# Three small edits to a hybrid decoder step: the pace of gating beside cross attention, the engine of one row scaling, the priority of one subtraction

## The chip, the cores and the metric

The kernel runs on one core of a Trainium2 chip. A core has five engines with instruction queues of their own: TensorE (PE, matrix products; PEld in the profile are its weight loads), VectorE (DVE), ScalarE (ACT), GpSimd (POOL) and SyncE (SP, which here only issues DMAs). Each engine works off its queue in order; semaphores make one wait for another. The metric is the time of one execution on the device in microseconds, as the median of several runs.

## The reference

One layer of a decoder, for a prompt of 1024 rows and for 8 samples with one new row each, all float32:

```python
# prompt
q, k, v, logf, u, z = mixer_inputs(rmsnorm(xp, g_mix), w_in, b_f, g_sgu_v)
xp = xp + merge_heads(fox_prompt(q, k, v, logf), sgu_prompt(u, z, w_s, b_s), g_att_out, g_sgu_out, w_o)
mk, mv = memory_kv(mem_prompt, g_mem, w_ck, w_cv)
xp = xp + cross_attend(rmsnorm(xp, g_cross), mk, mv, w_cq, w_co)
f, conv_p = conv_ffn(rmsnorm(xp, g_ffn), zeros, w_up, conv_w, conv_b, w_down)
y_prompt = rmsnorm(xp + f, g_final)
# samples: the same layer, with fox_sample over 8192 cached keys and values per sample
c = cumsum(concatenate([logf_cache, logf_new]))           # sums of the gates
s = q . k * 64 ** -0.5 + (c[query] - c[key])
att = softmax(s) @ v
```

The model width is 1024 and the feed-forward width 2816. Attention has 8 heads of 64, the spatial gating unit (`sgu`) 8 heads of 64 that mix the 128 rows of a chunk, and cross attention 4 heads of 256 over 256 memory rows. The gating unit computes u * (w_s z + b_s) for each chunk; its result is normed by rows, joins the attention output and goes through w_o.

## The kernel before

**Two streams.** The kernel is built as two Python generators. `prompt()` issues the work on the 1024 rows; `sample()` issues the decode of the 8 samples, whose caches are gathered page by page. Each `yield` of a number says how much PE time, roughly, has just been issued. A loop at the end of `build` adds these numbers up, and each time that a pace (`PACE`, by phase; 8.0 in the phase mid0) is reached, it issues one more step of the decode. While `held[0]` is set, no decode step is issued.

**Two halves.** The prompt is worked in two halves of 512 rows, four tiles of 128 rows each. The order is: input projection (`p1`), attention of half 0 and half 1, and then for each half: merge and output projection w_o, cross attention (`cross`), feed-forward (`ffn`). A product in float32 is made as three matmuls of high and low parts (`gemm3`, lines 272 to 274); `split` makes the parts, the high one on ACT (L235 or L238) and the low one on DVE (L236 or L239).

**Who sets the order.** The instructions are not run in the order in which the code issues them. A planner places them: it goes through the engines in modelled time and gives each engine the ready instruction with the first place in the code, as soon as a buffer for its result is free. Inside `with tc.high_priority():` an instruction gets a place ahead of all ordinary ones, so it is taken as soon as it is ready. `tc.issue_after(x)` and `behind(engine)` keep instructions behind another one of the same engine. The chip then runs each engine's list in that fixed order.

**Buffers.** Large row tiles come from `U`: 18 buffers of 128x1024 float32 values. The tiles of `xt` (4 buffers per half), the transposed and split inputs `hs` and `ls` (8), the query blocks `q2` (one per head), the probabilities `pp` (one per head), their transposes `pT`, and gating's `wst`, `z` and `u` all take one each. The bank `ms` of PSUM exists once (`MS`), and is shared by the decode and by attention.

**Gating.** `gating(hf)` computes the gating unit of one half in eight steps, each ending in `yield 1`. Steps one to three treat the first pair of chunks: the loads of w_s, z and u (L631, L638, L639), the scaling of z (L641), then twice four matmuls (L649) and four products with u (L659). Step four squares the first pair's rows on ACT (L230) and begins the second pair, with its loads; steps five and six are its matmuls and products; step seven squares its rows and makes the row factors (L222 on DVE, L223 on POOL); step eight scales the rows on DVE (L678) and stores them to `sgn_d` (L679). Half 0's gating runs beside attention. Half 1's runs beside half 0's cross attention, by `mix(cross(xt, sq), gating(1), 0.05)`: after each yield of d of the main stream, d times the ratio is added to an account, and gating steps are issued while it is above zero, each taking 1 off. What is left when the main stream ends is issued right behind it.

**Cross attention's yields.** `norm_T` yields 8 x 0.6 + 3 = 7.8, the query projections 8 x 5.2 = 41.6, the steps of the four heads 26, and `out_proj` 8 x 2.6 + 4 x 0.1 + 4 x 5.2 = 42: in all 117.4. In `cross`, the projection of the queries fills `q2` (L1226, ACT); `weigh` makes the scores (L1180), their maxima (L1182, DVE), the exponentials (L1188, ACT) and the scaling by the sums (L1193, ACT); `turned` and `gather` transpose the probabilities and multiply them with the memory values (L1200, L1208).

**The end of cross attention.** `out_proj` multiplies with w_co, column half by column half. In the second column half tiles 0 and 1 come one by one, tiles 2 and 3 together (L1082 to L1084). `residual` adds x (L1016, DVE) and squares the rows (L230, ACT); `factor` makes 1/rms of a tile (L1032 on ACT, L1033 on POOL). `both` then scales tiles 2 and 3 by their factors, half by half (L1045, L1046), for the transposes of the feed-forward's `norm_T` (L1116) and its first product (`gemm3_late`, L280 to L284). `both` is called once for each half of the prompt.

**The decode's gates.** For each sample, `gates_scan` sums the gates within a page and `gates` across pages: two small sums on PE into the bank `ms` (L1410), and on DVE a subtraction of 128x512 values (L1412) that reads this bank and writes `dec`. `soft_max` adds `dec` to the scores two steps later.

Of the kernel before, what the change touches and what calls it, by code (L numbers as in the profile page):

```python
# [11 lines left out]
AF = mybir.ActivationFunctionType  # L12
ALU = mybir.AluOpType
# [5 lines left out]
P = 128  # L19
# [59 lines left out]
def build(nc, tc, ctx, a, phases=None):  # L79
# [31 lines left out]
    def U(shape, dt=F32):  # L111
        n = 1
        for s in shape[1:]:
            n *= s
        t = upool.tile([P, UW], dt, tag="u", bufs=NU, name=nm("u"))[:, :n]
        if len(shape) == 3:
            t = t.rearrange("p (a b) -> p a b", b=shape[2])
        return t
# [7 lines left out]
    def sm(shape, tag, bufs=2, dt=F32):  # L126
        return small.tile(shape, dt, tag=tag, bufs=bufs, name=nm(tag))
# [136 lines left out]
    def wpair(w, kk, c0, n):  # L264

        return w[kk * 256 : (kk + 1) * 256, c0 : c0 + n].rearrange("(k p) n -> p k n", p=P)
# [742 lines left out]
    def squares():  # L1009
        return sm([P, 4, 2], "sqx", 2)  # L1010
# [13 lines left out]
    def out_proj(w, mh, ml, xt, fetch=None, ys=None):  # L1024

        sq = squares()
        part = sm([P, 4], "part", 2)

        def factor(i):

            r = sm([P, 1], f"fac{i}", 2)
            nc.scalar.activation(r, sq[:, i, 1:2], AF.Identity, scale=1.0 / D, bias=part[:, i : i + 1])  # L1032
            nc.gpsimd.tensor_tensor(r, r, mhalf[:, 0:1], op=ALU.pow)  # L1033
            return r

        def scaled(i, r):
            y = U([P, D])
            nc.scalar.activation(y, xt[i], AF.Copy, scale=r)
            return y

        def both(r2, r3):

            y2, y3 = U([P, D]), U([P, D])
            for c in (slice(0, 512), slice(512, D)):
                nc.scalar.activation(y2[:, c], xt[2][:, c], AF.Copy, scale=r2)  # L1045
                nc.scalar.activation(y3[:, c], xt[3][:, c], AF.Copy, scale=r3)  # L1046
            return [y2, y3]


        korder = (4, 5, 6, 7, 0, 1, 2, 3) if ys is None else tuple(range(8))  # L1050
        for n in range(2):
            ws = {}
            for kk in dict.fromkeys(k // 2 for k in korder):
                ws[kk] = wload(wpair(w, kk, n * 512, 512), 1024)
            if fetch and n == 0:
                xt += fetch()
            if n == 0:

                pss = [MM() for _ in range(4)]
                for k in korder:  # L1060
                    wh, wl = (ws[k // 2][q][:, k % 2, :] for q in range(2))
                    for i in range(4):
                        tb = slice(i * P, (i + 1) * P)
                        mmul(pss[i], mh[k][:, tb], wh, start=(k == korder[0]), stop=False)
                        mmul(pss[i], mh[k][:, tb], wl, start=False, stop=False)
                        mmul(pss[i], ml[k][:, tb], wh, start=False, stop=(k == korder[-1]))
                    yield 2.6
            if n == 0:
                for i in range(4):
                    residual(xt, sq, i, n, pss[i])  # L1070
                    if ys is not None:
                        nc.scalar.activation(part[:, i : i + 1], sq[:, i, 0:1], AF.Identity, scale=1.0 / D, bias=epsb)
                    yield 0.1
                continue

            for group in ((0,), (1,), (2, 3)):
                pss = [MM() for _ in group]
                for k in korder:
                    wh, wl = (ws[k // 2][q][:, k % 2, :] for q in range(2))
                    for i, ps in zip(group, pss):  # L1080
                        tb = slice(i * P, (i + 1) * P)
                        mmul(ps, mh[k][:, tb], wh, start=(k == korder[0]), stop=False)  # L1082
                        mmul(ps, mh[k][:, tb], wl, start=False, stop=False)
                        mmul(ps, ml[k][:, tb], wh, start=False, stop=(k == korder[-1]))  # L1084
                    if len(group) == 2 and k == korder[3]:
                        yield 5.2
                if ys is not None and group[0]:
                    ys.append(scaled(group[0] - 1, factor(group[0] - 1)))
                for i, ps in zip(group, pss):
                    residual(xt, sq, i, n, ps)  # L1090

                held[0] = len(group) == 2
                yield 5.2
        if ys is not None:
            with tc.high_priority():
                ys.append(partial(both, factor(2), factor(3)))
        return sq
# [268 lines left out]
    def decode():  # L1366
# [36 lines left out]
        def gates(b, A):  # L1403
            tot = sm([P, 8], "tot", 2)
            nc.vector.tensor_tensor(
                tot, A.rearrange("p (h k) -> p h k", k=64)[:, :, 63], lfz[:, b * 8 : b * 8 + 8], op=ALU.add
            )
            ps = MS()
            with behind(ENG.PE):
                mmul(ps[:, :8], suf, tot, start=True, stop=True)  # L1410
            dt_ = dec("dec").rearrange("p (k h) -> p k h", h=8)
            nc.vector.tensor_tensor(  # L1412
                dt_, ps[:, :8].unsqueeze(1).broadcast_to((P, 64, 8)), A.rearrange("p (h k) -> p k h", k=64), op=ALU.subtract
            )
            return dt_

        def kstep(b, ch, st):
# [99 lines left out]
        st, A, dt_, pm, dg, dv, vm = ([None] * 8 for _ in range(7))  # L1517
# [305 lines left out]
    def mix(main, bg, ratio):  # L1823

        t, more, res = 0.0, True, None
        while True:
            try:
                d = next(main)
            except StopIteration as e:
                res = e.value  # L1830
                break
            yield d
            t += d * ratio
            while more and t > 0:
                d = next(bg, None)
                more = d is not None
                if more:
                    t -= d
                    yield d
        if more:  # L1840
            yield from bg
        return res

    def prompt():
        def fill():
            yield from pmem()
            if not G0R:
                yield from gating(0)

        got, ahead = [], []  # L1850
        att1 = attention(1, lambda: got.append(merge_in(0)))
        att0, fill0 = attention(0, (lambda: next(att1)) if LT < 4 else None, LT), fill()

        def early():
            next(att0)
            next(fill0)

        yield from p1(early)
        phase[0] = "att0"
        att = yield from mix(att0, fill0, MIXR)  # L1860
        def load_x(hf):
            xt = []
            for i in range(4):
                t = U([P, D])
                nc.sync.dma_start(t, a["x"][(hf * 4 + i) * P : (hf * 4 + i + 1) * P, :])
                xt.append(t)
            return xt

        if LT > 3:
            yield next(att1)  # L1870
        ending = close(0, att)
        next(ending)
        phase[0] = "att1"
        ba_pool(True)
        if G0R:
            att = yield from mix(gating(0), att1, 1 / G0R)
        else:
            att = yield from beside(att1, ending, (0, 2))
        ba_pool(False)
        ending = close(1, att)  # L1880
        next(ending)
        ends = []
        for hf in range(2):
            if not got and hf == 0:
                got.append(merge_in(hf))
            xt = []
            phase[0] = f"mid{hf}"
            if hf == 0:
                mh, ml = yield from beside(merge(*got.pop()), ending, (3, 7))
            else:  # L1890
                mh, ml = yield from ahead[0]
            if ends:
                yield from ends.pop()
            sq = yield from out_proj(a["w_o"], mh, ml, xt, partial(load_x, hf))
            if hf == 0:
                ys = yield from mix(cross(xt, sq), gating(1), 0.05)
            else:
                ys = yield from cross(xt, sq)
            phase[0] = f"ffn{hf}"
            sq = yield from ffn(hf, xt, ys, (lambda: ahead.append(merge(*merge_in(1))) or ahead[0]) if hf == 0 else None)  # L1900
            held[0] = False
            ends.append(final(hf, xt, sq))
        yield from ends.pop()
# [121 lines left out]
```

## Time and profile before

| | |
|---|---|
| Median of 3 runs | 1798.12 us (1797.17, 1798.12, 1804.46) |
| Profiled execution | 1804.14 us, its span 1802.1 us |
| Instructions | 25097 |
| Mean granted clock of TensorE | 0.991 |
| Moved by DMA | 521.06 MB, mean 289 GB/s |

The span runs from the first to the last instruction of the profiled execution; all times in the profile are microseconds from its start unless marked ns. In rows of the timeline stand start, duration, engine, line, operation, out<-in by the program's names (buffer numbers left out), the shapes, the count, and in brackets how long the engine had stood idle before and what ended that. Where several equal instructions follow one another, the duration is that of all of them together. Rows with SPq are DMA issues. In the table of waits stand the total wait, the number of times, and the longest. Rows of a line's instructions give the shortest, median and longest duration in ns, the first and last start, and the shapes.

### The profile page before, as it was taken

The page shows a single profiled execution, that of the slowest core. Times are in us where ns is not written, and L with a number is a line of the kernel's source. Part 1 is how long each engine was busy: PE and PEld are TensorE (multiplying, and loading weights), DVE is VectorE, ACT ScalarE, POOL GpSimd, SP SyncE. Part 2 cuts the span into 40 slices and gives each one's busy share as a digit, 9 for nine tenths or more (in the row PEclk, how much of TensorE's full clock was granted, in tenths as well). Part 3 has the DMA queues.
Part 4 walks back from the last instruction along what each step waited for, and adds up shares of the span by engine and source line. Part 5 has one row for each costly group of instructions (what it writes and reads, how often), then busy time and mean ns, then how long its engine had stood idle before and what let it go on. Part 6 is the DMA issues. An engine that isn't in the chain of part 4 may idle for free.

```text
span 1802.1 us, 25097 instructions
## 1 busy us (share of the span) xinstructions
PE 1737.0 (96%) x9637; PEld 1287.2 (71%) x9637; DVE 1398.2 (78%) x1729; ACT 736.4 (41%) x1378; POOL 506.6 (28%) x461
## 2 busy tenths in 40 slices
PE   8999999878999999999999999999989999999997
PEld 5887777555677667777777777776666778767875
DVE  4689658988788986999999999887875549855344
ACT  6332265465643635333333244336353323332332
POOL 1252333433123332332322223343422112002110
PEclk9999999999999999999999999999999999999999
DMA  8886888786697985778788778988879687568982
GB/s 296 301 298 226 300 317 329 265 273 212 223 407 277 355 331 217 290 291 341 296 305 309 290 302 321 377 304 325 308 276 338 224 297 249 185 260 299 357 312 82
DMA packets 157074, 521.06 MB, mean 289 GB/s; under 512 B 20874, under 2 KB 40842, under 8 KB 124186
## 3 DMA queue, kind: packets, MB, share of 16 engines
q0 software_dynamic: 57168, 341.14, 49.8%
q1 hardware_dynamic: 92874, 165.73, 26.7%
q10 hardware_dynamic: 6912, 12.59, 1.9%
q8 instruction: 76, 1.25, 0.3%
q14 instruction: 44, 0.36, 0.1%
HBM read 495.47 MB, written 23.93 MB: 288 GB/s over the span
## 4 chain that ended last, share of the span: by engine, by line
PE 47%; DMA 11%; issue 8%; DVE 6%; POOL 2%; ACT 1%; POOLq 0%; DVEq 0%
DMA kv<-cache_v,io 7%; PE ba L272 6%; PE ba L274 6%; PE ba L273 6%; PE dv L1488 3%; PE bb L272 3%; PE bb L274 3%; PE bb L273 3%; DMA kv<-cache_k,io 2%; DVE s L1440 2%; DVE kv L1436 1%; PE dv L331 1%; PE dv L1764 1%; POOL kv L1482 1%; POOL kv L1420 1%
## 5 line engine op out<-in xcount | busy, mean ns | idle before, releaser
L235 ACT ACTIVATE wh<-wr 128x1024 fp32r<-128x1024 f32 (+2 forms) x220 | 228.9, 1044 | 421.5 <-PE ba L273 138.8
L236 DVE TENSOR_TENSOR wl<-wr,wh 128x1024 fp32r<-128x1024 f32 (+2 forms) x220 | 262.9, 1199 | 172.6 <-PE ba L274 57.7
L1420 POOL DMA_INDIRECT kv<-cache_k,io x128 | 199.2, 1556 | 570.9 <-DVE s L1440 325.3
L1436 DVE TENSOR_TENSOR kv<-kv,d 128x1024 f32<-128x1024 f32 (+1 forms) x156 | 258.1, 1681 | 24.7 <-DMA kv<-cache_k,io 24.7
L1440 DVE TENSOR_REDUCE s<-kv 128x16 f32<-128x1024 f32 (+1 forms) x156 | 258.1, 1672 | 0.0
L1482 POOL DMA_INDIRECT kv<-cache_v,io x128 | 168.5, 1317 | 254.9 <-PE dv L1488 177.5
L272 PE MATMUL ba<-u,wh 128*128 128x512 f32 x528 | 209.3, 397 | 0.0
L273 PE MATMUL ba<-u,wh 128*128 128x512 f32 x528 | 208.8, 396 | 0.5 <-DVE u L239 0.5
L274 PE MATMUL ba<-u,wl 128*128 128x512 f32 x528 | 208.8, 396 | 0.0
L272 PE MATMUL ba<-wh,u 128*128 128x512 f32 (+1 forms) x495 | 186.4, 379 | 2.6 <-ACT u L235 2.6
L273 PE MATMUL ba<-wl,u 128*128 128x512 f32 (+1 forms) x495 | 185.1, 375 | 1.2 <-DVE wl L236 1.2
L274 PE MATMUL ba<-wh,u 128*128 128x512 f32 (+1 forms) x495 | 183.2, 375 | 0.0
L1488 PE MATMUL dv<-kv,s 128*32 128x512 f32 x1024 | 127.7, 606 | 3.6 <-DMA kv<-cache_v,io 3.5
L272 PEld LDWEIGHTS ba<-u,wh 128*128 128x128 f32 x528 | 99.5, 188 | 27.2 <-issue 5.6
L274 PEld LDWEIGHTS ba<-u,wl 128*128 128x128 f32 x528 | 99.3, 188 | 26.5 <-issue 4.0
L273 PEld LDWEIGHTS ba<-u,wh 128*128 128x128 f32 x528 | 99.3, 188 | 25.8 <-issue 3.1
L272 PEld LDWEIGHTS ba<-wh,u 128*128 128x128 f32 x495 | 93.0, 188 | 27.0 <-issue 6.5
L272 PE MATMUL bb<-u,wh 128*128 128x512 f32 x272 | 108.7, 400 | 0.0
L274 PE MATMUL bb<-u,wl 128*128 128x512 f32 x272 | 107.8, 397 | 0.0
L273 PE MATMUL bb<-u,wh 128*128 128x512 f32 x272 | 107.6, 396 | 0.0
L273 PEld LDWEIGHTS ba<-wl,u 128*128 128x128 f32 x495 | 93.0, 188 | 20.0 <-DVE wl L236 1.9
L274 PEld LDWEIGHTS ba<-wh,u 128*128 128x128 f32 x495 | 92.9, 188 | 19.5 <-issue 1.6
(445 smaller groups left out, 3313.8 us busy)
## 6 DMA issues: line engine op xcount, KB each, us to landing
wr<-w_up SPq DMA_DIRECT2D x88, 512.0 KB
kv<-w_up POOLq DMA_DIRECT2D x22, 1024.0 KB, 7.6
wr<-w_down SPq DMA_DIRECT2D x40, 512.0 KB
kv<-w_down POOLq DMA_DIRECT2D x11, 1024.0 KB, 8.3
wr<-w_in SPq DMA_DIRECT2D x16, 512.0 KB
wr<-w_o SPq DMA_DIRECT2D x16, 512.0 KB
wr<-w_cq SPq DMA_DIRECT2D x16, 512.0 KB
wr<-w_co SPq DMA_DIRECT2D x16, 512.0 KB
```

Source lines behind the costliest of these rows:

```text
L235: nc.scalar.activation(h, src, AF.Copy)
L236: nc.vector.tensor_tensor(l, src, h.bitcast(F32), op=ALU.subtract)
L272: mmul(out, sh, mh, start=(i == 0), stop=False)
L273: mmul(out, sh, ml, start=False, stop=False)
L274: mmul(out, sl, mh, start=False, stop=(i == n - 1))
L331: mmul(ps[32 * j : 32 * j + 32, :w], xT[:, k, :] if nk == 8 else xT[:, k * 8 : k * 8 + 32], raw[:, q, j * w : (j + 1) * w], start=(k == 0) ...
L1420: nc.gpsimd.indirect_dma_start(kv, None, a["cache_k"], off(kidx[:, b, ch : ch + 1]))
L1436: nc.vector.tensor_tensor(kvv[:, i : i + m, :], kvv[:, i : i + m, :], qb.unsqueeze(1).broadcast_to((P, m, 512)), op=ALU.mult)
L1440: nc.vector.tensor_reduce(s[:, ch * 4 + i : ch * 4 + i + m, :].rearrange("p k h -> p (k h)"), kvv[:, i : i + m, :].rearrange("p k (h d) -> ...
L1482: nc.gpsimd.indirect_dma_start(kv, None, a["cache_v"], off(kidx[:, b, ch : ch + 1]))
L1488: mmul(dv[32 * j : 32 * j + 32, :], s[:, ch * 4 : ch * 4 + 4, :].rearrange("p k h -> p (k h)"), kvv[:, j, :], start=(ch == 1), stop=(ch == ...
L1764: mmul(ps[32 * j : 32 * j + 32, :P], xsT[:, k, :], rvs[j // 2][:, k, j % 2, :], start=(k == 0), stop=(k == 7), tile_position=(0, 32 * j),)
```

## The change

In `both`, tile 3's rows are scaled by a `tensor_scalar` on VectorE instead of an `activation` on ScalarE; tile 2's stay on ScalarE. In `gates`, the subtraction is issued under `tc.high_priority()`. In `prompt`, the ratio at which half 1's gating is mixed into half 0's cross attention goes from 0.05 to 0.09. No operation is added or left out.

```diff
             y2, y3 = U([P, D]), U([P, D])
             for c in (slice(0, 512), slice(512, D)):
                 nc.scalar.activation(y2[:, c], xt[2][:, c], AF.Copy, scale=r2)
-                nc.scalar.activation(y3[:, c], xt[3][:, c], AF.Copy, scale=r3)
+                nc.vector.tensor_scalar(y3[:, c], xt[3][:, c], r3, None, op0=ALU.mult)
             return [y2, y3]
@@ gates
             dt_ = dec("dec").rearrange("p (k h) -> p k h", h=8)
-            nc.vector.tensor_tensor(
-                dt_, ps[:, :8].unsqueeze(1).broadcast_to((P, 64, 8)), A.rearrange("p (h k) -> p k h", k=64), op=ALU.subtract
-            )
+            with tc.high_priority():
+                nc.vector.tensor_tensor(
+                    dt_, ps[:, :8].unsqueeze(1).broadcast_to((P, 64, 8)), A.rearrange("p (h k) -> p k h", k=64), op=ALU.subtract
+                )
             return dt_
@@ prompt
             if hf == 0:
-                ys = yield from mix(cross(xt, sq), gating(1), 0.05)
+                ys = yield from mix(cross(xt, sq), gating(1), 0.09)
             else:
                 ys = yield from cross(xt, sq)
```

## The prediction

> **What bounds the kernel now.** I read the busy shares first.
>
> ```profile
> PE 1737.0 (96%) x9637; PEld 1287.2 (71%) x9637; DVE 1398.2 (78%) x1729; ACT 736.4 (41%) x1378; POOL 506.6 (28%) x461
> ```
>
> TensorE (PE) works for 1737.0 of a 1802.1 us span. The change alters none of its matmuls, so it can only touch the 65 us in which PE stands, and the time in which PE runs at a lowered clock. Next, who PE waited for (total us, times, longest):
>
> ```profile
> PE ba L807 <- ACT wr L817: 6.8, 6, 1.9
> ...
> PE ms L852 <- DVE dec L1412: 2.7, 1, 2.7
> ...
> PE bb L1116 <- ACT u L1046: 1.1, 1, 1.1
> PE ba L1116 <- ACT u L1045: 1.1, 1, 1.1
> ```
>
> L1412 is the subtraction that gets priority; it has eight executions, and one of them ever holds PE. L1046 is the scaling that moves to VectorE (DVE); it holds PE once. L1045, its sister for the third tile, stays on ScalarE (ACT), so its 1.1 us is not addressed. Last, the stages of the two ends of cross attention (busy us of PE, PEld, DVE, ACT, POOL, then the granted clock, DMA share, GB/s):
>
> ```profile
> 701.00:704.40 3.40, 2.87 (x11) 2.15 (x12) 0.65 (x2) 3.40 (x10) 1.27 (x2) 0.50 1.02 427
> 704.40:707.80 3.40, 3.40 (x19) 3.40 (x18) 2.53 (x6) 1.39 (x4) 0.28 (x1) 0.53 0.99 401
> ...
> 1339.00:1342.40 3.40, 1.52 (x14) 1.33 (x13) 1.93 (x3) 2.62 (x7) 0.54 (x1) 0.99 1.01 417
> 1342.40:1345.80 3.40, 3.40 (x17) 3.21 (x16) 1.82 (x5) 2.44 (x9) 0.00 (x0) 0.51 0.51 210
> ```
>
> In 1339 to 1342.4 PE stands 3.40 - 1.52 = 1.88 us, and the next 3.4 us run at 0.51 of the clock, which costs another 3.4 x 0.49 = 1.7 us. Idle time at these ends is paid nearly twice. In 701 to 704.4 ACT is busy for the whole 3.40 us: it is the engine that sets the pace there.
>
> **The change, part by part.** *A, priority for L1412.* The one place where it matters, in attention:
>
> ```profile
> 313.35 0.34 PE L1410 MATMUL ms<-tot,cp 128*128 128x8 f32 x2
> ...
> 313.41 0.68 DVE L1427 TENSOR_TENSOR kv<-kv,d 128x512 f32<-128x512 f32 x1
> ...
> 314.00 1.22 DVE L236 TENSOR_TENSOR wl<-wr,wh 128x1024 fp32r<-128x1024 f32 x1
> ...
> 315.14 0.55 DVE L813 TENSOR_REDUCE mx<-ba 128x1 f32<-128x384 f32 x1
> 315.61 1.02 DVE L1412 TENSOR_TENSOR dec<-ms,d 128x512 f32<-128x512 f32 x1
> 315.72 0.58 ACT L814 ACTIVATE t<-ba,mx 128x384 f32<-128x384 f32 x1 [0.78 <-DVE mx L813]
> ...
> 316.68 0.87 PE L852 MATMUL ms<-t,u 128*64 128x256 f32 x8 [2.72 <-DVE dec L1412]
> 317.48 0.55 PE L836 MATMUL bb<-cp,t 128*128 128x128 f32 x3
> ```
>
> The sum is ready at 313.69; L1412 comes behind L236 and L813. With priority it can start when L1427 ends, 314.09, and end at 315.11, so L852 starts 1.5 us sooner. But L236 and L813 are then 1.02 us later, so the exponential L814 too: from 315.72 to about 316.74, ending 317.3. Its transposes L836 are next on PE, at 317.48 now, hardly sooner then. What is late next is the softmax maximum. Bounds: -1.5 (the planner lets L813 pass L236 too) to +1.0 (it starts behind L236 as now, and only L813 slips). I take -0.5, nearer the loss of the gain, because L813 reads the row of the next score block. The other seven executions have no PE wait in the list above: 0, as DVE does the same work in another order; the split L236 that they push back by 1.0 us is covered by weight tiles split ahead.
>
> *B, the fourth tile's rows on DVE.* First the end near 700:
>
> ```profile
> 701.71 0.61 ACT L230 ACTIVATE junk<-u 128x512 bf16<-128x512 f32 x1
> ...
> 701.88 0.54 POOL L1033 TENSOR_TENSOR fac<-fac,mhalf 128x1 f32<-128x1 f32 x1 [1.63 <-ACT fac L1032]
> ...
> 702.68 0.62 ACT L230 ACTIVATE junk<-u 128x512 bf16<-128x512 f32 x1
> ...
> 703.29 1.32 ACT L1046 ACTIVATE u<-u,fac 128x512 f32<-128x512 f32 x2
> ...
> 703.42 1.91 PE L284 MATMUL ba<-u,wh 128*128 128x256 f32 x8
> ...
> 704.72 1.68 DVE L678 TENSOR_SCALAR u<-u,r4r 128x512 f32<-128x512 f32 x4 [1.12 <-POOL r4r L223]
> ...
> 705.13 1.48 PE L1116 MATMUL ba<-cp,u 128*128 128x128 f32 x6
> ```
>
> L678 is the same operation, shape and type as the new scaling: 1.68 / 4 = 0.42 us each, where ACT takes 1.32 / 2 = 0.66. The factor is ready at 702.42. On DVE, idle in most of that window, the rows are done at 702.42 + 0.84 = 703.3 instead of 704.61. But PE has L284 until 705.33 and starts the transposes L1116 right behind it: the wait is already covered. Gain between 0 and 1.3 us; I take 0.3.
>
> The end near 1340 has no such cover:
>
> ```profile
> 1339.91 0.54 POOL L1033 TENSOR_TENSOR fac<-fac,mhalf 128x1 f32<-128x1 f32 x1 [2.39 <-ACT fac L1032]
> ...
> 1341.12 1.32 ACT L1046 ACTIVATE u<-u,fac 128x512 f32<-128x512 f32 x2
> ...
> 1341.88 0.33 PE L1116 MATMUL bb<-cp,u 128*128 128x128 f32 x1 [1.10 <-ACT u L1046]
> ```
>
> The factor is ready at 1340.45, ACT takes it at 1341.12 and the first half is out at 1341.78. On DVE it is out near 1340.6 + 0.42 = 1341.0, so PE resumes 0.8 us sooner (bounds 0, if DVE runs another reduction first, to 1.0). The 1.88 us of idle falls to about 1.1; whether the half-rate stretch goes with it is open, 0 to 1.7, and I take half, 0.85. By the Trainium skill, "TensorE: Matmul & The Clock Gate", section "Why this matters for your kernels", only idle gaps over about 3 us bring the clock down. Here 1.88 us in pieces of at most 1.10 did, so the trace contradicts it; by that rule there is nothing to win from the clock and the sum would be 0.85 worse.
>
> The Trainium skill's "SBUF — State Buffer", section "SBUF: two separate sides", speaks against B: a VectorE operation in two-port mode locks GpSimd out of writing DMA descriptors. No gather ran beside L678, so no run here shows it. As an estimate from L678's row, four scalings of 0.42 us would hold gathers back by 1.7 us at most.
>
> *C, the ratio 0.05 to 0.09.* Gating has eight steps of cost 1; the stage it lies beside is worth some 117 us, so 0.05 grants 5.9 steps and the last two fall after its end, and 0.09 grants all eight, the last at 78 of the 117. What leaves the end near 700: two squares on ACT (0.61 and 0.62 above), the four scalings L678 and two stores. The squares held L1046 by 703.29 - 702.42 = 0.87 us, which B removes anyway; DVE's 1.68 fell beside L1116 on PE. Worth 0.2 (0 to 0.5); the lowered clock of 701 to 707.8 I leave as it is (upper bound of its loss to be won: 3.4). What enters is earlier work in the softmax stretch:
>
> ```profile
> L659 DVE SCALAR_TENSOR_TENSOR u<-ba,gp,u x16: 334/343/351, 557.0 to 675.9; 128x128 f32<-128x128 f32 x16
> ...
> L641 DVE SCALAR_TENSOR_TENSOR u<-u,rz,xg x4: 740/746/751, 549.0 to 635.7; 128x512 f32<-128x512 f32 x4
> ...
> 600.00:640.00 40.00, 38.01 (x183) 22.70 (x182) 37.22 (x47) 29.87 (x76) 14.19 (x11) 1.00 0.95 360
> ```
>
> (That window's DVE is 93% busy.) Two L641, four L659 and the squares are 1.5 + 1.4 + 1.2 = 4.1 us; PE, 95% busy there, hides most behind queued matmuls, and loses all of it if that cover is gone. Bounds 0 to +4.1; I take +0.5.
>
> **Sum.** -0.5 - 0.3 - 0.8 - 0.85 - 0.2 + 0.5 = -2.2 us on the profiled execution (1804.1 us with 1802.1 us of span, 6 us above the median of the runs, 1798.1). Carried to the median: 1796. Lower bounds -1.5 - 1.3 - 1.0 - 1.7 - 0.5 - 3.4 = -9.4, upper +1.0 + 4.1 = +5.1: the likeliest case alone is 1789 to 1803.
>
> **Rivals.** *1, gating takes the buffers of the softmax (slower).* All of cross attention's rows lie in 18 row buffers. Rows that show they are short (the first four from ACT's timeline, the last two from SP's):
>
> ```profile
> 591.76 0.56 ACT L1188 ACTIVATE u<-ba,cbs,rq 128x256 f32<-128x256 f32 x1 [0.76 <-PE bb L1180]
> ...
> 598.14 0.60 ACT L1226 ACTIVATE u<-ba 128x512 f32<-128x512 f32 x1 [1.26 <-PE ba L649]
> 598.79 1.71 ACT L1193 ACTIVATE u<-u,cr 128x256 f32<-128x256 f32 x4
> ...
> 609.20 0.60 ACT L1226 ACTIVATE u<-ba 128x512 f32<-128x512 f32 x1 [0.54 <-PE ba L274]
> 605.52 3.82 SPq L249 DMA_DIRECT2D wr<-w_co  x2
> ...
> 616.30 0.42 SPq L638 DMA_DIRECT2D u<-zg_d  x1
> ```
>
> The copy of a query block at 598.14 waited for L649, gating's last read of its z: it needed that buffer. Gating's second pair of rows is loaded at 616.30, when the projections are over. At 0.09 the pair comes at 34 of the 117 instead of 60, before the last projection (609.20), and outranks the probabilities of head 0 (591.76) and head 1. These then wait until the projections free their inputs. A head's exponentials and scaling take 4 x 0.56 + 1.71 = 3.9 us of ACT; one or two heads move behind 609 (3.9 to 7.8), with up to two half-rate stretches (3.4), and a load that waits for a buffer holds SP's next loads of w_co, 609.2 - 605.5 = 3.7. In all 3.9 to 14.9, say 9.5; without the +0.5 the rest is -2.7: 1805. It decides if L638's second load issues before about 595. Against it: z's own buffer comes free sooner too.
>
> *2 and 3, attention is reordered.* The planner places every instruction by priority, and the second L1412 stands at the head of attention:
>
> ```profile
> sum 180.00, PE 153.46 PEld 108.85 DVE 152.56 ACT 103.57 POOL 59.94; mean PE 25.58 PEld 18.14 DVE 25.43 ACT 17.26 POOL 9.99
> ```
>
> That is 300 to 480 us: 26.5 us of PE idle, mostly softmax waits (L817 above) that depend on which DVE operation goes first. A third of it either way is 8.8, with one half-rate stretch 10.5: 1798.1 - 2.2 - 10.5 = 1785 for the better, and 1798.1 - 1.7 + 10.5 = 1807 (A's gain gone) for the worse. For: DVE is 85% busy there. Against: one of 1.02 us is moved.
>
> *4, nothing arrives.* The planner already placed all three well, or the next wait takes every gain: 1798. It lies inside the likeliest case's range and shares its chance.
>
> **How the numbers follow.** Likeliest case (with rival 4) 0.45, rival 1 0.25, rival 2 0.16, rival 3 0.14. A measurement of this kernel can tell about 0.5%, 9 us, from no change: faster means under 1789.1, slower over 1807.1. Faster: most of rival 2 (0.15) and the edge of the likeliest case (0.03), 0.18. Slower: a bit under half of rival 1 (0.11) and over half of rival 3 (0.09), 0.20. Same: 0.62. The range 1784 to 1810 holds the bounds of the likeliest case and most of each rival.
>
> **What would show it.** A: the wait of L852 for L1412 gone, and L836 or L814 behind it no earlier than 317.3. B: the scaling on DVE near 0.42 us, no PE wait for the fourth tile near 1340, and full clock right after, or half as now. C: no squares of gating and no stores of sgn_d at the end near 700; the second load of zg_d before 600, with L1188 first starting after 600, would be rival 1. PE idle in 300 to 480 well off 26.5 us would be rival 2 or 3. I am wrong if the median leaves 1784 to 1810, or if the time moved in a stage that no edit touches.

## The result and the profile after

The changed kernel is slightly slower: a median of 1808.15 us (12 runs, 1806.05 to 1813.23) against 1801.05 us for the kernel before in the same comparison (12 runs), a ratio of 1.0036 with an interval of 1.0023 to 1.0049. On the 1798.1 us that the prediction started from, that is 1804.6 us. The profiled execution has a span of 1806.3 us. From L1413 on, every line number is one higher than before (L1412 is now L1413, L1440 is L1441). Busy shares, from the page:

```profile
PE 1740.7 (96%) x9637; PEld 1288.4 (71%) x9637; DVE 1398.7 (77%) x1733; ACT 731.9 (41%) x1374; POOL 500.0 (28%) x461
```

TensorE has the same 9637 instructions. From the table of waits (total us, times, longest):

```profile
DVE u L641 <- DMA u<-zg_d: 5.2, 1, 5.2
...
PE ms L852 <- DVE dec L1413: 2.7, 1, 2.7
```

The wait that the priority was to shorten is there as before, 2.7 us. A new one heads the list: VectorE stands for 5.2 us before L641, the scaling of gating's z, because the load of zg_d has not landed. The timeline of the moment (SP, DVE, ACT, POOL, PE):

```profile
581.18 0.74 SPq L638 DMA_DIRECT2D u<-zg_d  x1
593.41 0.37 SPq L639 DMA_DIRECT2D u<-sgu_d  x1
593.82 0.47 SPq L1390 DMA_DIRECT2D d<-qs_d  x1
...
590.06 0.68 DVE L1182 TENSOR_REDUCE cmx<-bb 128x2 f32<-128x512 f32 x1
595.96 1.41 DVE L641 SCALAR_TENSOR_TENSOR u<-u,rz,xg 128x512 f32<-128x512 f32 x2 [5.22 <-DMA u<-zg_d]
...
599.31 0.68 DVE L1182 TENSOR_REDUCE cmx<-ba 128x2 f32<-128x512 f32 x1
599.91 2.35 DVE L1437 TENSOR_TENSOR kv<-kv,d 128x1024 f32<-128x1024 f32 x2
...
611.28 0.17 DVE L1191 RECIPROCAL cr<-cl 128x4 f32<-128x4 f32 x1
...
602.47 0.57 ACT L1188 ACTIVATE u<-bb,cbs,rq 128x256 f32<-128x256 f32 x1 [1.97 <-PE ba L1180]
...
607.05 0.94 POOL L1421 DMA_INDIRECT kv<-cache_k,io  x1 [11.84 <-DVE s L1441]
...
613.33 1.53 PE L1200 MATMUL ba<-cp,u 128*128 128x128 f32 x4 [2.02 <-ACT u L1193]
```

The decode's product and the first reciprocal L1191 before:

```profile
590.15 2.41 DVE L1436 TENSOR_TENSOR kv<-kv,d 128x1024 f32<-128x1024 f32 x2
...
598.59 0.16 DVE L1191 RECIPROCAL cr<-cl 128x4 f32<-128x4 f32 x1
```

Read it as a queue. The load goes out at 581.18 and its data are used at 595.96, 14.8 us later. L641 has been at the head of VectorE's list since 590.7. Behind it stand the second maximum of head 0 (L1182, 599.31), the decode's products with its keys (L1437, at 599.91 instead of 590.15) and, behind those, the reciprocal L1191 for head 0's probabilities, at 611.28 instead of 598.59. TensorE has run out of other work at 611.31 and waits 2.02 us. Ten-microsecond windows (busy us of PE, PEld, DVE, ACT, POOL, granted clock, DMA share, GB/s), before, then after, aligned to the start of cross attention:

```profile
590.10:600.10 10.00, 10.00 (x51) 8.50 (x49) 10.00 (x13) 5.28 (x16) 5.74 (x3) 1.00 0.75 307
600.10:610.10 10.00, 10.00 (x58) 7.04 (x57) 10.00 (x15) 9.41 (x23) 4.59 (x3) 1.00 0.81 278
610.10:620.10 10.00, 9.06 (x44) 5.02 (x42) 10.00 (x12) 7.38 (x19) 3.75 (x2) 1.00 1.01 392
```

```profile
591.00:601.00 10.00, 10.00 (x55) 7.48 (x44) 4.89 (x7) 0.73 (x4) 2.85 (x3) 1.00 1.01 407
601.00:611.00 10.00, 10.00 (x58) 7.08 (x57) 10.00 (x11) 6.20 (x15) 1.88 (x2) 1.00 0.40 135
611.00:621.00 10.00, 6.17 (x20) 4.21 (x19) 10.00 (x14) 8.09 (x21) 6.40 (x2) 0.76 1.00 378
```

VectorE loses 5 us in the first window (4.89 busy, 10.00 before). In the second the DMA share falls to 0.40, as the next gather of keys (L1421) waits 11.84 us for VectorE's sums L1441 to free its buffer. In the third TensorE stands 3.83 us and its clock falls to 0.76. TensorE's own work in this stretch has hardly changed (878 and 877 matmuls), so the stretch can be measured by what is lost in it: idle time plus time lost to the half-rate clock. From the first L1116 of cross attention to the last L1116 of the feed-forward's start, before and after:

```profile
530.10:707.50 177.40, 172.98 (x878) 126.22 (x877) 152.16 (x194) 84.91 (x187) 63.88 (x44) 0.98 0.84 317
```

```profile
531.00:715.50 184.50, 176.08 (x877) 127.67 (x876) 152.38 (x194) 82.36 (x184) 58.37 (x44) 0.97 0.82 309
```

Idle: 177.40 - 172.98 = 4.4 and 184.50 - 176.08 = 8.4 us. With 3.4 and 5.1 us lost to the clock, the loss goes from 7.8 to 13.5 us. The second half's cross attention and feed-forward start, where B works, lose 17.5 us before (11.6 idle, 5.9 clock) and 11.6 after (9.9, 1.7).

### The profile page after: what moved, and what is told of

The parts are those of the page before. It is cut to its first block, busy times and chain, and to the rows that moved or that the text cites. A ratio compares the mean times of both kernels' runs of the same rounds, so it can differ in the third digit from the quotient of the medians.

```text
span 1806.3 us, 25092 instructions
## 1 busy us (share of the span) xinstructions
PE 1740.7 (96%) x9637; PEld 1288.4 (71%) x9637; DVE 1398.7 (77%) x1733; ACT 731.9 (41%) x1374; POOL 500.0 (28%) x461
## 4 chain that ended last, share of the span: by engine, by line
PE 50%; issue 8%; DMA 8%; DVE 6%; POOL 2%; ACT 2%; POOLq 0%; DVEq 0%; SPq 0%
PE ba L272 7%; PE ba L274 6%; PE ba L273 6%; DMA kv<-cache_v,io 6%; PE dv L1489 4%; PE bb L272 3%; PE bb L274 3%; PE bb L273 3%; DVE kv L1437 1%; DVE s L1441 1%; PE dv L331 1%; PE dv L1765 1%; PE ba L1066 1%; PE ba L1083 1%; PE ba L1084 1%
## 5 line engine op out<-in xcount | busy, mean ns | idle before, releaser
L236 DVE TENSOR_TENSOR wl<-wr,wh 128x1024 fp32r<-128x1024 f32 (+2 forms) x220 | 262.4, 1198 | 172.7 <-PE ba L274 58.3
L1421 POOL DMA_INDIRECT kv<-cache_k,io x128 | 187.2, 1462 | 570.8 <-DVE s L1441 323.7
L1437 DVE TENSOR_TENSOR kv<-kv,d 128x1024 f32<-128x1024 f32 (+1 forms) x156 | 258.0, 1680 | 25.3 <-DMA kv<-cache_k,io 25.2
L1441 DVE TENSOR_REDUCE s<-kv 128x16 f32<-128x1024 f32 (+1 forms) x156 | 257.9, 1672 | 0.0
L1483 POOL DMA_INDIRECT kv<-cache_v,io x128 | 174.4, 1362 | 263.2 <-PE dv L1489 188.8
L274 PE MATMUL ba<-u,wl 128*128 128x512 f32 x544 | 215.8, 397 | 0.0
L272 PE MATMUL ba<-u,wh 128*128 128x512 f32 x544 | 215.8, 397 | 0.0
L273 PE MATMUL ba<-u,wh 128*128 128x512 f32 x544 | 215.3, 396 | 0.5 <-DVE u L239 0.5
L1489 PE MATMUL dv<-kv,s 128*32 128x512 f32 x1024 | 127.6, 605 | 5.1 <-DMA kv<-cache_v,io 5.1
L272 PEld LDWEIGHTS ba<-u,wh 128*128 128x128 f32 x544 | 102.5, 189 | 28.1 <-issue 4.8
L273 PEld LDWEIGHTS ba<-u,wh 128*128 128x128 f32 x544 | 102.5, 188 | 25.6 <-issue 2.3
L272 PE MATMUL bb<-u,wh 128*128 128x512 f32 x256 | 102.1, 399 | 0.0
L273 PE MATMUL bb<-u,wh 128*128 128x512 f32 x256 | 101.6, 397 | 0.0
L274 PE MATMUL bb<-u,wl 128*128 128x512 f32 x256 | 101.3, 396 | 0.0
```

The lines of the kernel that those rows point to most:

```text
L236: nc.vector.tensor_tensor(l, src, h.bitcast(F32), op=ALU.subtract)
L272: mmul(out, sh, mh, start=(i == 0), stop=False)
L273: mmul(out, sh, ml, start=False, stop=False)
L274: mmul(out, sl, mh, start=False, stop=(i == n - 1))
L1421: nc.gpsimd.indirect_dma_start(kv, None, a["cache_k"], off(kidx[:, b, ch : ch + 1]))
L1437: nc.vector.tensor_tensor(kvv[:, i : i + m, :], kvv[:, i : i + m, :], qb.unsqueeze(1).broadcast_to((P, m, 512)), op=ALU.mult)
```

## The experiments

The edits to gating's timing use `mix_at`, which issues gating step n once more than times[n] of cross attention's 117 has been issued; 0.09 corresponds to the times 0, 11, 22, 33, 44, 56, 67, 78. The table collects the stretch defined above (us from each kernel's profile), the stand of VectorE before the second pair's L641, and the ratio of the whole to the kernel before. In the expectations, theory 1 and theory B are rival 1 of the prediction; "rival 2" there is gating's own work in the softmax stretch and "rival 3" a cost of A or B, not the prediction's rivals of those numbers.

Each kernel has one profile, so a loss has its own spread: in the five kernels with the second pair at its old place (before, e2, e7, and e16 and e17 below) it runs from 6.2 to 7.8 us, mostly by how many half-rate stretches fell into it; the idle time alone runs from 4.0 to 4.7.

| kernel | length | PE idle | lost to clock | loss | stand at L641 | ratio, whole kernel |
|---|---|---|---|---|---|---|
| before | 177.4 | 4.4 | 3.4 | 7.8 | 0 | 1 |
| after | 184.5 | 8.4 | 5.1 | 13.5 | 5.2 | 1.0036 [1.0023, 1.0049] |
| e1 | 185.2 | 8.4 | 6.3 | 14.7 | 5.3 | 1.0048 [1.0030, 1.0067] |
| e2 | 176.5 | 4.6 | 1.6 | 6.2 | 0 | 1.0009 [0.9991, 1.0027] |
| e3 | 180.4 | 9.0 | 1.7 | 10.7 | 0 | 1.0020 [1.0003, 1.0037] |
| e4 | 186.1 | 10.1 | 6.4 | 16.5 | 5.3 | 1.0043 [1.0025, 1.0060] |
| e5 | 174.1 | 5.2 | 0 | 5.2 | 3.5 | 0.9975 [0.9961, 0.9989] |
| e6 | 177.3 | 4.8 | 3.3 | 8.1 | 0.9 | 1.0015 [1.0001, 1.0029] |
| e7 | 177.1 | 4.2 | 3.4 | 7.6 | 0 | 1.0018 [1.0003, 1.0033] |
| e8 | 187.8 | 13.6 | 5.1 | 18.7 | 5.6 | 1.0097 [1.0075, 1.0118] |
| e9 | 190.4 | 16.1 | 8.5 | 24.6 | 0 | 1.0075 [1.0053, 1.0096] |
| e10 | 182.1 | 7.1 | 3.2 | 10.3 | 0 | 1.0069 [1.0049, 1.0088] |
| e13 | 186.2 | 11.0 | 4.9 | 15.9 | 7.0 | 1.0102 [1.0081, 1.0123] |
| e14 | 182.2 | 6.7 | 4.7 | 11.4 | 0 | 1.0070 [1.0047, 1.0093] |
| e15 | 177.1 | 6.5 | 1.6 | 8.1 | 0 | 0.9997 [0.9979, 1.0016] |

### Which part costs: e1 and e2

e1 is the kernel before with the ratio alone, e2 the changed kernel without it.

```diff
-                ys = yield from mix(cross(xt, sq), gating(1), 0.05)
+                ys = yield from mix(cross(xt, sq), gating(1), 0.09)
```

> The kernel before with the ratio 0.09 alone. Theory 1 (gating's second pair of chunks takes two of the 18 row buffers before the query projections are over, the probabilities of heads 0 and 1 wait, and PE stands in the softmax): the whole loss is here, +6 to +10 us against before, first exponential L1188 near 602 as in the changed kernel. Rival 2 (gating's own work on ACT and DVE now lies in the softmax stretch): the same, +6 to +10. Rival 3 (the scaling on DVE or the priority costs the time): 0 to +2 us.

> The changed kernel with the ratio back at 0.05: the scaling on DVE and the priority alone. Theory 1 and rival 2: -3 to +1 us against before, since both edits touch only the two ends of cross attention and the order of one subtraction. Rival 3: +4 to +8 us, as the changed kernel.

The ratio alone costs 0.48% (8.7 us), A and B together change nothing that can be told. The loss is C's.

### Which step of gating: e3, e4, e6

All three have A and B, and steps one to three as at 0.09. e3 moves only step four (the second pair's loads and scaling) to 49.5. e4 leaves step four early and moves steps five to eight to the places that they had before the change. e6 does both.

```diff
-                ys = yield from mix(cross(xt, sq), gating(1), 0.09)
+                ys = yield from mix_at(cross(xt, sq), gating(1), (0.0, 11.1, 22.2, 49.5, 44.4, 55.6, 66.7, 77.8))    # e3
+                ys = yield from mix_at(cross(xt, sq), gating(1), (0.0, 11.1, 22.2, 33.3, 80, 100, 120, 120))          # e4
+                ys = yield from mix_at(cross(xt, sq), gating(1), (0.0, 11.1, 22.2, 49.5, 80, 100, 120, 120))          # e6
```

> The changed kernel, all gating steps at the times of 0.09, but step four, which loads the second pair of chunks, not before 49.5 of the 117 of issued work, when the last projection is issued; steps five to eight stay at their times. Theory 1: the loss goes, -3 to +2 us against before, and L1188 first starts near 592 again. Rival 2: the loss stays, +5 to +9 us, for the second pair's products, squares and scalings still lie in the softmax stretch. A store of sgn_d that waits in SP's queue as the cause: also +5 to +9 us, for it stays too.

> The changed kernel, steps one to four at the times of 0.09, steps five to eight at those of 0.05 (the second pair loaded early, its work done late, the last two steps behind cross attention). Theory 1: +5 to +10 us against before. Rival 2, and a store of sgn_d that holds SP's queue: -2 to +2 us, for none of that work lies in the softmax stretch.

> The changed kernel with gating's steps one to three as at 0.09, step four (second pair) not before 49.5 of 117, steps five and six at 80 and 100, seven and eight behind the end as before the change. Against the kernel with step four late alone (1.0020 [1.0003, 1.0037]) it moves steps five to eight out of the softmax stretch. Theory 1 (early second pair costs 6 to 9 us, the rest nothing): ratio 0.999 to 1.002 for both. Theory 2 (gating's products, squares, scalings and stores in the softmax stretch cost the remaining 3 to 4 us): this one comes back to 1.000 to 1.001 and the PE idle of the stage falls from 7.1 to about 2 us.

e4 and e6 differ in the time of step four alone. The stretch loses 16.5 us in the one and 8.1 in the other, and the ratios are 1.0043 and 1.0015. So the early second pair is what costs, some 8 us where it happens, about 5 of them (0.28%) left in the whole kernel. e3 keeps the steps behind the pair in the softmax stretch and loses 2.6 us more than e6 there; over the whole kernel its 1.0020 can't be told from e6's 1.0015. So far all of this fits rival 1.

### Row buffers: e7 and e8

A 19th row buffer, paid for with two small tiles; e7 is the kernel before with it, e8 the changed kernel with it.

```diff
-NU = 18
-NT = 7
+NU = 19
+NT = 6
...
-        return dpool.tile([P, 512], dt, tag="d2", bufs=5, name=nm("d2"))[:, :n]
+        return dpool.tile([P, 512], dt, tag="d2", bufs=4, name=nm("d2"))[:, :n]
```

> A control: the kernel before with 19 row buffers instead of 18, paid for by one small tile of 128x512 each less in two other pools (7 to 6 and 5 to 4). All theories: within 0.5% of the kernel before; what the two smaller pools cost is read here.

> The changed kernel with the same 19 row buffers, to be set against the control. Theory 1 (early second pair takes row buffers from the softmax): one of the two buffers in dispute is given back, so at least half of the loss goes, ratio to the control under 1.002, and L1188 first starts under 66 us after cross attention begins (71.5 with 18 buffers, 61.7 before the change). Theory 2 (not buffers but gating's work on DVE, ACT or in SP's queue): the ratio to the control stays 1.0035 or more, and L1188 starts as late as with 18.

Rival 1's account of the loss fails here. Issues of SP and the scaling, from e8's timeline:

```profile
583.39 0.59 SPq L638 DMA_DIRECT2D u<-zg_d  x1
584.02 0.54 SPq L639 DMA_DIRECT2D u<-sgu_d  x1
...
595.08 0.56 ACT L1188 ACTIVATE u<-bb,cbs,rq 128x256 f32<-128x256 f32 x1 [2.23 <-PE ba L1180]
...
597.90 1.42 DVE L641 SCALAR_TENSOR_TENSOR u<-u,rz,xg 128x512 f32<-128x512 f32 x2 [5.56 <-DMA u<-zg_d]
```

The second load follows the first at once, where it was held until 593.41, and L1188 starts 62.5 us after cross attention begins (71.5 without the buffer). The hold that rival 1 blamed is gone, and the stretch loses 18.7 us, more than the 13.5 without the buffer. (Of its 13.6 us of idle, 4.03 are a wait of the decode's matmul L1489 for its values; without them the loss would still be 14.7.) The stand of VectorE is still there, 5.56 us. e7 adds that a late L1390 in SP's queue costs nothing by itself: it comes at 592.91 there, about as late as in the changed kernel (593.82; before: 581.43), and the stretch loses 7.6 us, no more than before. The whole of e8 is at 1.0097 where the changed kernel is at 1.0036; 0.0018 of that is the control's, and the rest is not explained.

### The stand: e9, e10, e13, e14

These keep the early load and move L641 alone: it is issued with the next step and kept behind VectorE's newest instruction of that moment. Line numbers behind it are 8 higher in e9, e10 and e14.

```diff
+            def scaled():
+                with tc.issue_after(newest(ENG.DVE)) if hf and pr_ else nullcontext():
                     for i in range(2):
                         nc.vector.scalar_tensor_tensor(
                             z[:, i, :], z[:, i, :], rz[:, t0 + i : t0 + i + 1], gsv, op0=ALU.mult, op1=ALU.mult
                         )
+            if not (hf and pr_):
+                scaled()
             yield 1
             for q in range(2):
+                if hf and pr_ and q == 0:
+                    scaled()
```

e9 is the changed kernel with it, e10 is e4 with it.

> The changed kernel, with the same early load of the second pair, but its scaling on VectorE (L641) issued one gating step later and kept behind the newest VectorE instruction of that moment: some 26 places later in VectorE's list, the order of the others kept. In the four slow kernels so far VectorE stood 5.2 to 5.6 us before L641 for the load of zg_d. Theory W (that stand, with the decode's products queued behind it, is what pushes VectorE's work into the softmax): the stand is gone, VectorE is busy for over 7 of the ten us at 591 to 601 (4.89 now), L1188 and the scalings of head 0 come sooner, ratio 0.999 to 1.002. Theory B (row buffers taken early hold the probabilities, and SP's queue): L639 is held until near 593 as now, the ratio stays 1.0035 or more.

> As the kernel with the second pair early and steps five to eight late (1.0043 [1.0025, 1.0060]), but L641 is issued with step five and kept behind the newest VectorE instruction: the load still takes its buffers at 33 of 117, and nothing of gating falls into the softmax but that load. Theory W: as the kernel with the pair at 49.5 (1.0015 [1.0001, 1.0029]) or better, and no stand before L641. Theory B: 1.0035 or more, with the buffers held longer than before.

Both ratios went the wrong way, and the traces say why. In e9 the move made a new wait. From its table of waits (L657 is gating's matmul, L644 the scaling):

```profile
PE bb L657 <- DVE u L644: 9.1, 1, 9.1
```

TensorE's list has gating's matmuls in a place that now comes before their input, so e9 tells nothing of the stand. e10, whose matmuls come later, has no such wait: the loss in the stretch falls from e4's 16.5 to 10.3 us. But the second half's cross attention, which the edit doesn't touch, loses 24.0 us (e4: 13.7), and its instructions stand in another order; why the planner changed it was not tested. There, from the timeline (ACT, then PE; with the 8 taken off, L1175 is the key copy L1167, PE's L1188 the scores L1180, L1201 the scaling L1193):

```profile
1255.43 1.70 ACT L1201 ACTIVATE u<-u,cr 128x256 f32<-128x256 f32 x4 [0.21 <-DVE cr L1199]
1261.48 1.06 ACT L235 ACTIVATE wh<-wr 128x1024 fp32r<-128x1024 f32 x1 [4.35 <-DMA wr<-w_co]
1262.45 0.58 ACT L1234 ACTIVATE u<-bb 128x512 f32<-128x512 f32 x1
1262.92 0.59 ACT L1175 ACTIVATE t<-ba 128x512 f32<-128x512 f32 x1
1263.40 0.60 ACT L1209 ACTIVATE u<-ba 128x512 f32<-128x512 f32 x1
...
1263.57 2.93 PE L1188 MATMUL ba<-t,u 128*128 128x256 f32 x6 [8.61 <-ACT t L1175]
```

It is the same accident on another engine: ScalarE stands 4.35 us before a split of w_co whose data haven't landed, the key copy L1175 stands behind it, and TensorE waits 8.61 us.

e13 and e14 are e4 and e10 with the 19 buffers of e7, so that all four combinations are there.

> The kernel with the second pair early and steps five to eight late, now with 19 row buffers (paid for as in the control, which lost 0.2% and nothing in the stage from the first L1116 of cross attention to the last of the feed-forward's start: 177.2 us there, 177.4 before). With 18 buffers that stretch takes 186 us. The load is no longer held, but VectorE still stands before L641. Theory W alone or W and B together: 183 to 189 us in that stretch, a stand of over 5 us before L641. Theory B alone: 177 to 180.

> The same with 19 row buffers and L641 kept behind, so neither the held load nor the stand is there. With 18 buffers and L641 behind the stretch took 182.1 us: 4 of the 8.7 us that the early load costs were gone. If the rest is the buffers' (theory W and B together): 177 to 179 us. If the rest is neither's: 181 to 184. The total may lie above that, as the order of the second half's cross attention differed in the kernel with 18 (a PE wait of 8.6 us there).

VectorE's rows of e13, then of e14, in the same place:

```profile
595.05 0.68 DVE L1182 TENSOR_REDUCE cmx<-bb 128x2 f32<-128x512 f32 x1
602.75 1.42 DVE L641 SCALAR_TENSOR_TENSOR u<-u,rz,xg 128x512 f32<-128x512 f32 x2 [7.02 <-DMA u<-zg_d]
...
606.69 2.35 DVE L1437 TENSOR_TENSOR kv<-kv,d 128x1024 f32<-128x1024 f32 x2
```

```profile
594.59 0.68 DVE L1190 TENSOR_REDUCE cmx<-bb 128x2 f32<-128x512 f32 x1
596.92 0.69 DVE L1511 TENSOR_TENSOR d<-dv,cp 128x512 f32<-128x512 f32 x1 [1.65 <-PE dv L1497]
...
599.23 2.35 DVE L1445 TENSOR_TENSOR kv<-kv,d 128x1024 f32<-128x1024 f32 x2
```

Without the stand the decode's products start 599.23 - 594.59 = 4.6 us behind the maximum instead of 11.6. TensorE's waits in the softmax, from e4, e10, e13 and e14 (in e10 and e14, L1208, L1188, L1201 and L1175 are L1200, L1180, L1193 and L1167 of the others):

```profile
614.93 1.64 PE L1200 MATMUL ba<-cp,u 128*128 128x128 f32 x8 [2.95 <-ACT u L1193]
618.80 1.63 PE L1208 MATMUL ba<-cp,u 128*128 128x128 f32 x8 [0.47 <-ACT u L1201]
...
622.19 3.78 PE L1180 MATMUL bb<-t,u 128*128 128x256 f32 x8 [5.94 <-ACT t L1167]
624.12 1.99 PE L1188 MATMUL ba<-t,u 128*128 128x256 f32 x8 [0.31 <-ACT t L1175]
```

Without the stand these waits fall from 2.95 to 0.47 us and from 5.94 to 0.31. Others stay or come: a wait of 2.2 us for L1167 is in e4 and e10 alike, and e14 has one of 3.3 us for an exponential. The losses of the stretch:

| | stands at L641 | L641 behind |
|---|---|---|
| 18 row buffers | 16.5 (e4) | 10.3 (e10) |
| 19 row buffers | 15.9 (e13) | 11.4 (e14) |

The stand is worth 6.2 and 4.5 us, the buffer 0.6 and -1.1. In idle time alone, which leaves out the clock, the stand is worth 3.0 and 4.3 us, the buffer -0.9 and 0.4. With 19 buffers the whole kernel agrees: 1821.51 us with the stand, 1814.05 without, ratios 1.0102 and 1.0070. With 18 it does not, for the reordered second half covers the gain. Against e6's 8.1 us, 2.2 to 3.3 us of the early pair's cost remain without the stand; they are not explained. The second of the two buffers that the pair takes, which no run gave back, could hold some of it. The length of the stretch alone could not have shown this: it also holds more or less of the decode's work.

### Other ratios, and the parts alone: e5, e11, e12, e15, e16, e17

e5 and e15 are the changed kernel at 0.06 and 0.07; e11 is the kernel before at 0.06, e12 that with B; e16 is B alone, e17 A alone, both at 0.05.

```diff
-                ys = yield from mix(cross(xt, sq), gating(1), 0.05)    # e11, e12; 0.09 in e5 and e15
+                ys = yield from mix(cross(xt, sq), gating(1), 0.06)    # e5, e11, e12; 0.07 in e15
```

> The changed kernel with a ratio of 0.06: all eight steps of gating fall inside cross attention, as at 0.09, but the second pair is loaded after about 50 of the 117 and the last step comes at 117. Theory 1 (the early load of the second pair costs, nothing else does): no loss, ratio 0.998 to 1.001, L1188 first starts near 61 us after cross attention begins as it does before. Theory 2 (any gating work between the scores and the end costs, wherever it is put): ratio 1.002 to 1.005, as with 0.09. Theory 3 (the end near 700 with no decode step's work left costs): ratio about 1.002, and the PE gaps sit at the feed-forward's start.

> The kernel before with a ratio of 0.06 and nothing else. With parts A and B it was 0.9975 [0.9961, 0.9989], and A and B alone 1.0009 [0.9991, 1.0027]. If the gain is the ratio's, 0.996 to 0.998 here; if it needs B's quicker rows at the ends, 0.999 to 1.001.

> A ratio of 0.06 and the fourth tile's rows on VectorE, without the priority of L1412. If the priority costs (rival 3, 0.1 to 0.3%), this is 0.995 to 0.997, under the kernel with all three at 0.9975; if it does nothing, 0.9975 as there.

> The changed kernel with a ratio of 0.07: step four comes at 43 of 117, after the next sample's query load in SP's queue but ahead of w_co. 0.06 gave 0.9975, 0.09 gave 1.0036. If what counts is whether the pair's load goes out while the projections still run, and the scaling is placed before the data are there: a stand before L641 of over 2 us and 1.000 to 1.004; if the place behind the query load is enough: 0.997 to 0.999.

> The kernel before with part B alone. The prediction's sum gives B 0.3 near 700 and 0.8 + 0.85 near 1340, 1.95 us of 1801: ratio 0.9989. At the ratio 0.06, B took it from 0.9999 to 0.9981, 0.0018. If the sum is right 0.998 to 1.000; if the freed place on ScalarE turns the order of the second half's cross attention for the worse, 1.001 or more.

> The kernel before with part A alone. The prediction gave it -0.5 us (-1.5 to +1.0), 0.9997. In the changed kernel the first three L1412 have the places they had before, so if A does only what its places show: 0.999 to 1.001, and the 2.7 us wait of L852 is there. If the later ones reorder the decode (rival 3, another order of later stages): 1.001 to 1.003, in a stage after 550 us.

With A and B the ratio goes 1.0009 at 0.05, 0.9975 at 0.06, 0.9997 at 0.07 and 1.0036 at 0.09. e5, at 0.06, beats both kernels: 1800.65 us against 1803.21, 4.5 us by the ratio. The gain isn't the pace's: 0.06 alone (e11) is 0.9999 [0.9983, 1.0016]. It seems to be mostly B's: with B alone (e16) 0.9981 [0.9963, 0.9998], with B at 0.06 (e12) 0.9981 [0.9964, 0.9998]. A alone (e17) is 1.0010 [0.9995, 1.0024], no change that can be told. But B beside A at 0.05 (e2) is 1.0009 [0.9991, 1.0027], and none of B's gain shows there. In e2's trace the end near 1340 stands in another order than in e16, with TensorE waits of 1.17 and 1.27 us and 6.8 us at half rate. The intervals of e2 and e16 overlap, so whether A takes B's gain at 0.05 is open; at 0.06 it does not (e5 against e12). At 0.07, the load goes out at 601.89 behind the query load, L641 comes at 610.39 without a stand, and the loss of the stretch is 8.1 us: that agrees with what decides being whether VectorE reaches L641 before its data. Rows of e5:

```profile
614.75 0.67 SPq L638 DMA_DIRECT2D u<-zg_d  x1
...
628.19 1.42 DVE L641 SCALAR_TENSOR_TENSOR u<-u,rz,xg 128x512 f32<-128x512 f32 x2 [3.45 <-DMA u<-zg_d]
```

and e5's window around it:

```profile
624.40:634.40 10.00, 10.00 (x54) 6.66 (x47) 6.52 (x10) 6.45 (x22) 1.90 (x2) 1.00 1.03 412
```

Here VectorE stands too, 3.45 us, and TensorE is busy for the whole of those ten microseconds. A stand costs by what is queued behind it; here the exponentials of three of the four heads are already done.

## Why the prediction was wrong

The sum was -2.2 us (1796); on its basis the changed kernel is at 1804.6, 6.5 us the other way.

**The step that failed is the term for what enters the softmax stretch in C**: "PE, 95% busy there, hides most behind queued matmuls ... I take +0.5", bounded at +4.1. It counted the busy time of the operations that move in (and of the second pair's eight products L659 only four, 1.4 us too little). What cost was a wait of one of them: L641 sits in VectorE's fixed list, and the load it needs takes 14.8 us beside the decode's gathers, while the list brings VectorE to it after 9.6 (581.18 to 590.74). C alone measured +8.7 us, +4.9 beside A and B (1.0036 against 1.0009), where the sum had +0.3. That the stand is most of this is shown by e4, e10, e13 and e14, which issue gating's later steps later than the changed kernel does; on the changed kernel itself the one test, e9, made a wait of its own. Neither a bound nor a rival held that wait.

**Rival 1** gave 1805 us, and the time on the prediction's basis is 1804.6. Its sign came too: L638 at 581.18 (it named 595), L639 held until 593.41, L1188 at 602.47. But its mechanism is not what cost most, and that its number came out is luck. With a buffer more the load isn't held and the first exponentials come early, and the loss stays (e8, e13). A sign that fits is no proof of the cause that predicted it.

**A** does nothing in the place for which it was made. The subtraction is where it was, with L236 and L813 ahead of it, as the changed kernel's DVE rows and then its PE row show:

```profile
313.79 1.22 DVE L236 TENSOR_TENSOR wl<-wr,wh 128x1024 fp32r<-128x1024 f32 x1
314.93 0.55 DVE L813 TENSOR_REDUCE mx<-ba 128x1 f32<-128x384 f32 x1
315.39 1.02 DVE L1413 TENSOR_TENSOR dec<-ms,d 128x512 f32<-128x512 f32 x1
...
316.47 1.55 PE L852 MATMUL ms<-t,u 128*64 128x256 f32 x8 [2.72 <-DVE dec L1413]
```

The same 2.7 us wait is in e17, A alone. The -0.5 was taken for a move that didn't happen; why the planner didn't make it was not tested. Later A does move something: in e17 the fourth subtraction starts at 682.53, between two of the decode's products, where before it came behind both (683.58), and VectorE's order differs from there on. What that is worth can't be told from e17's 1.0010. Rivals 2 and 3, a reordered attention, are out: up to about 553 us no instruction of PE, DVE or ACT changed its place.

**B** agrees with its size within a wide interval: 1.95 us predicted, 0.9981 [0.9963, 0.9998] measured alone (3.4 us, 0.4 to 6.7). At the end near 1340, in the changed kernel:

```profile
1346.94 0.54 POOL L1033 TENSOR_TENSOR fac<-fac,mhalf 128x1 f32<-128x1 f32 x1 [2.38 <-ACT fac L1032]
...
1347.52 0.88 DVE L1046 TENSOR_SCALAR u<-u,fac 128x512 f32<-128x512 f32 x2 [0.26 <-POOL fac L1033]
1348.06 0.33 PE L1116 MATMUL bb<-cp,u 128*128 128x128 f32 x1 [0.57 <-DVE u L1046]
```

and its windows there:

```profile
1343.40:1346.80 3.40, 2.36 (x18) 1.86 (x16) 2.41 (x7) 2.47 (x6) 0.78 (x1) 1.00 1.01 419
1346.80:1350.20 3.40, 2.31 (x18) 2.05 (x19) 3.14 (x8) 2.23 (x7) 0.54 (x1) 1.00 1.00 419
```

A half of the rows takes 0.44 us (0.42 was read off L678), the first comes 0.5 us behind the factor instead of 1.3, and TensorE's wait is 0.57 instead of 1.10. The half-rate stretch is gone too (1.00 in both windows, 0.51 before), but that can't be put down to B. In e16, with B alone, almost the same waits (0.75, 0.78 and 0.57 us) are followed by 3.4 us at half rate, from 1334.7 to 1338.1:

```profile
1334.34 0.33 PE L1116 MATMUL bb<-cp,u 128*128 128x128 f32 x1 [0.57 <-DVE u L1046]
...
1332.80:1336.20 3.40, 2.05 (x12) 1.94 (x12) 2.86 (x6) 1.90 (x6) 0.54 (x1) 0.77 1.02 426
```

So the 0.85 that the sum took for the clock is not shown to be B's, and that it came here was in part luck; the last section says what decides it. The rule cited there from the Trainium skill, "TensorE: Matmul & The Clock Gate", section "Why this matters for your kernels", no idle gaps over about 3 us, is not enough here: 1.88 us of idle in pieces of at most 1.10 was followed by the half rate before, and pieces of at most 0.78 us were in e16.

**C's end near 700** went as said, the squares, scalings and stores are gone from it, and what that saves is small beside what was lost ahead of it. The half-rate stretch there is shorter (6.8 us before, 3.4 after), but with C alone (e1) it is 6.8 as before.

## What to carry to other kernels

When a load is moved earlier, move its first consumer in your mind too: in a queue that runs in fixed order, the consumer's place is a promise about when the data land, and whatever is queued behind it pays if the promise is broken. Read the landing time off the same traffic (here 14.8 us for 512 KB, with the DMA share at 1.01), not off a quiet moment, and put the consumer behind work that is sure to be ready. When a rival's outward sign appears, still take its cause away in an experiment before believing it.

## What the runs showed of the hardware

With 18 row buffers all kernels run the same lists up to the end of attention, and yet cross attention began at 530.1 to 538.9 us in their profiles, with 3.4 to 17.1 us lost to half-rate stretches that come in lengths of 3.4 us or a multiple. That is as much as the whole effect studied here, so stages were compared behind that point, and the verdicts rest on medians.

The length of a wait doesn't say whether half rate follows. Waits of 0.73, 0.78 and 0.57 us in the changed kernel (1344 to 1348) were not followed by it, and almost the same waits in e15 and e16 were. The traces show what differs. In each of the 19 profiles every half-rate stretch starts a whole number of periods of 3.413 us after the first one (within 0.02 us), so there is a grid of windows of 3.413 us, which lies elsewhere from profile to profile. What counts is TensorE's idle time within one such window. Of the windows at full clock (without the first and last 20 us of a profile), none of 9339 with less than 1.2 us of idle was followed by half rate, 80 of 229 with 1.2 to 2.0 us were, and all 55 with 2.0 us or more. In e16 the three waits put 1.8 us into one window; in the changed kernel the grid cuts them into 0.9 and 1.2 us. So a wait of TensorE has a second cost that is partly luck: it depends on what other waits share its window.
